# Residual rows added at each slot's down product instead of gathered by group, with fixed buffers and independent scatters

## The chip, the cores and the metric

The kernel runs on one core of one Trainium2 chip. The metric is device time in microseconds of one execution; the time given for a kernel is the median of its runs. A profile is taken of one execution, and its span is a little shorter than that execution's time.

## What is computed

One layer of a hybrid encoder over 512 tokens of width 1024, then a final RMSNorm. The first two parts (a gated mix of chunk-causal attention and pooling, then cross attention to 256 memory tokens) are dense. The third is a hierarchical mixture of experts, and this is where the change lies. Each token picks one of 4 groups and then the two best of that group's 8 experts; there are 32 experts.

```python
def hierarchical_moe(xn, w_rg, b_rg, w_re, b_re, w_gate, w_up, w_down):
    group_prob = jax.nn.softmax((xn @ w_rg) + b_rg, axis=-1)
    g_w, g_idx = lax.top_k(group_prob, 1)
    ...
    weights = g_w * e_w
    ...
    for e in range(N_EXPERTS):
        hid = jax.nn.silu(xn @ w_gate[e]) * (xn @ w_up[e])
        out = out + (hid * cw[..., e:e + 1]) @ w_down[e]
    return out

    h = h + hierarchical_moe(rms_norm(h, ffn_norm_g[l]), ...)
    return rms_norm(h, final_norm_g)
```

All is in float32. Each expert has 3 MB of weights (gate and up 2 MB, down 1 MB).

## The kernel before

The program is written out in full in Python, without loops on the chip, and each engine runs its instructions in the order in which the code issues them. On chip, memory is split into arenas (H, Q, E, G, J, C, B, R of pairs in rounded float32, F and W of plain float32). The dense stages take buffers from them; as they end, arenas are turned into slots of 1 MB for expert weights (`e_slots`, `to_raw`). Weights are fetched in the order of their use as slots come free (`e_load`, called by `e_done`), all from SyncE's queue.

The eight PSUM banks are a list: `bank()` takes the first one (L208), `put()` appends to the end (L211). The bank of a step is put back as soon as its last reader is issued; the wait for that reader is then with whoever writes the bank next.

The dense stages leave the residual h as rows of 1024 in DRAM (`H3`). The router gives lists: `src` (for each pair of experts, the tokens of its 128 places, 64 for each expert), `cws` (their weights), `srank` (the place of each within its group) and `gsrc` (for each group, the tokens of its 256 places, as two tiles t of 128). Places that hold no token are left out by the gathers' and scatters' bound.

`experts()` goes over p = 0..15, a pair of experts each (4 pairs make a group, PG = 4):

- `gather(p)` (L1534) fetches the pair's token rows from `H3` into `XG[p % 2]` with a DMA issued by GpSimd.
- `take(p)` (L1540) transposes them on TensorE, 8 blocks in two banks, into `XS[p % 2]`: the first four are copied out by VectorE (L1554), the other four by ScalarE (L1552). `rstd(p)` (L1559) squares the rows on ScalarE into two junk banks, then three small steps on GpSimd; it ends by issuing `gather(p + 2)`.
- `up(p)` (L1572) is 16 matmuls of 512 columns (two experts side by side), then SiLU on ScalarE (L1588) and a product on VectorE (L1589).
- `places(p)` (L1593) makes the one-hot matrix `OH` on GpSimd. `turn(p)` (L1598) transposes the hidden values.
- `down(p)` (L1608) is two halves n of 8 matmuls. Each half is split into a high part (ScalarE, L228) and a low part (VectorE, L229), `Y`, scaled by `cws`.
- `add(p, n)` (L1631) adds `Y` through `OH` into four banks `acc[t, n]`, which are held over the group's four pairs.

In the pair p the order is up(p), places(p), take(p + 1), add(p - 1, 0), turn(p), rstd(p + 1), add(p - 1, 1), down(p). Once in a group (p = 4, 8, 12), after add(p - 1, 1), `sums` (L1674) adds the residual rows in `HG` to the four acc banks and squares them; after down, `output` (L1682) scales by the norm and the gain and scatters the rows, one scatter for each t. `residual` (L1645) has gathered the residual rows of a group into `HG` with two DMAs after down(p) with p % 4 == 1. In the last group the residual is added by four matmuls with the identity instead (L1740), ahead of down(15), and add, square, scale and scatter follow half by half (L1750 to L1759).

## Time and profile before

| | us |
|---|---|
| median of 3 runs (lowest, highest) | 758.93 (757.88, 759.64) |
| the profiled execution | 759.05 |
| its span in the profile | 757.3 |

```profile
PE 717.7 (95%) x3603; PEld 499.9 (66%) x3604; DVE 393.9 (52%) x726; ACT 326.8 (43%) x652; POOL 183.7 (24%) x263
q1 hardware_dynamic: 30960, 144.73, 50.4%
q0 software_dynamic: 4896, 10.50, 3.8%
```

The first line gives for each engine its busy time, its share of the span and its instructions: PE is TensorE's matmuls, PEld its weight loads, DVE VectorE, ACT ScalarE, POOL GpSimd. The others give for a DMA queue its packets, megabytes and the share of the 16 DMA engines; q1 carries the weights, q0 what GpSimd issues. A matmul's end is modelled, so TensorE's busy share isn't its share of peak. The experts run from about 509 us to the end.

### The profile page before, as it was taken

To read this page: it belongs to the slowest core of one execution; us is meant where nothing else is said; L and a number is where in the kernel's file an instruction comes from. 1 tells how busy PE (TensorE), PEld (TensorE's weight loads), DVE (VectorE), ACT (ScalarE), POOL (GpSimd) and SP (SyncE) were. 2 spreads that over 40 slices of the span, in tenths; PEclk is the share of its full clock that TensorE was granted. 3 is DMA by queue.
4 is the path that set the end of the run, shared out by engine and by line. 5 is a ranking of instruction groups with operands and counts; after the bars stand their busy time and mean duration, and the time that the engine had idled before them with its cause. 6 is when DMAs were issued, how large, how long until landed. Compare 5 with 4: busy or idle time off the path is not lost. (4 is left out here: it accounts for less than half of the span.)

```text
span 757.3 us, 9883 instructions
## 1 busy us (share of the span) xinstructions
PE 717.7 (95%) x3603; PEld 499.9 (66%) x3604; DVE 393.9 (52%) x726; ACT 326.8 (43%) x652; POOL 183.7 (24%) x263
## 2 busy tenths in 40 slices
PE   8999999999999889999999999969999999998892
PEld 6787788868778668899898888833434444444330
DVE  6948444677878594886455454352224225215112
ACT  7543322656665654553444344323333424324211
POOL 4566000111111142410000002224233422512312
PEclk9999999999999999999999999979999999999997
DMA  9231323211130442256451078779999999999940
GB/s 329 85 106 28 115 87 106 79 57 39 38 112 29 151 161 106 83 166 194 141 203 57 29 310 357 251 268 346 420 419 418 419 418 418 417 417 422 412 168 36
DMA packets 38211, 159.34 MB, mean 210 GB/s; under 512 B 6544, under 2 KB 9360, under 8 KB 26640
## 3 DMA queue, kind: packets, MB, share of 16 engines
q1 hardware_dynamic: 30960, 144.73, 50.4%
q0 software_dynamic: 4896, 10.50, 3.8%
q10 hardware_dynamic: 2304, 3.45, 1.3%
q8 instruction: 29, 0.48, 0.3%
q14 instruction: 22, 0.18, 0.1%
HBM read 160.75 MB, written 6.29 MB: 221 GB/s over the span
## 5 line engine op out<-in xcount | busy, mean ns | idle before, releaser
L229 DVE SCALAR_TENSOR_TENSOR B<-b,zs,B 128x512 fp32r<-128x512 f32 x32 | 23.8, 750 | 72.2 <-ACT B L228 72.2
L1589 DVE SCALAR_TENSOR_TENSOR F<-b,r3s,F 128x256 f32<-128x256 f32 x16 | 7.7, 483 | 95.9 <-ACT F L1588 95.9
L1588 ACT ACTIVATE F<-b,r3s 128x256 f32<-128x256 f32 x16 | 7.6, 475 | 106.9 <-PE b L1580 106.9
L1636 PE MATMUL b<-B 128*128 128x512 f32 x128 | 37.7, 416 | 2.2 <-ACT B L228 1.7
L236 PE MATMUL b<-H,R 128*128 128x512 f32 x92 | 36.7, 399 | 0.0
L228 ACT ACTIVATE B<-b,zs 128x512 fp32r<-128x512 f32 x32 | 21.9, 686 | 33.2 <-PE b L1618 32.4
L1580 PE MATMUL b<-H,F 128*64 128x512 f32 x112 | 29.4, 593 | 2.0 <-DMA H<-in_we 2.0
L425 PE MATMUL b<-H,Q 128*128 128x512 f32 x120 | 27.5, 390 | 1.0 <-ACT Q L223 1.0
L751 ACT ACTIVATE F<-b,sm,cc_q 128x128 f32<-128x128 f32 (+3 forms) x32 | 19.8, 619 | 19.6 <-DVE sm L750 18.0
L1636 PEld LDWEIGHTS b<-B 128*128 128x128 f32 x128 | 21.6, 189 | 8.1 <-issue 2.6
L234 PE MATMUL b<-H,G 128*128 128x512 f32 x60 | 25.4, 423 | 1.3 <-ACT H L223 1.3
L425 PEld LDWEIGHTS b<-H,Q 128*128 128x128 f32 x120 | 22.5, 188 | 6.1 <-ACT Q L223 1.5
L1566 POOL TENSOR_SCALAR ssx<-ssx 128x1 f32<-128x1 f32 x16 | 4.1, 256 | 90.8 <-ACT b L1564 90.5
L1580 PE MATMUL b<-R,F 128*64 128x512 f32 x88 | 25.2, 593 | 0.0
L235 PE MATMUL b<-H,G 128*128 128x512 f32 x60 | 24.4, 407 | 0.7 <-DVE H L226 0.7
L1199 POOL TENSOR_TENSOR F<-F 128x512 f32<-128x512 f32 x6 | 8.1, 1342 | 66.3 <-ACT F L1197 66.3
L1580 PE MATMUL b<-Q,F 128*64 128x512 f32 x72 | 23.5, 620 | 0.0
L223 ACT ACTIVATE E<-W 128x1024 fp32r<-128x1024 f32 (+3 forms) x24 | 18.9, 797 | 9.8 <-PE b L235 3.6
L1547 PEld LDWEIGHTS b<-ident,F 128*128 128x128 f32 x128 | 13.7, 140 | 14.0 <-issue 11.4
L226 DVE TENSOR_TENSOR R<-W,R 128x1024 fp32r<-128x1024 f32 (+2 forms) x15 | 20.0, 1342 | 4.8 <-ACT R L223 4.8
L1580 PEld LDWEIGHTS b<-H,F 128*64 128x64 f32 x112 | 9.3, 137 | 18.5 <-issue 15.4
L223 ACT ACTIVATE G<-W 128x1024 fp32r<-128x1024 f32 (+3 forms) x20 | 17.7, 883 | 8.7 <-PE b L235 3.6
(619 smaller groups left out, 2243.0 us busy)
## 6 DMA issues: line engine op xcount, KB each, us to landing
W<-in_wd SPq DMA_DIRECT2D x61, 512.0 KB, 3.5
H<-in_we SPq DMA_DIRECT2D x20, 1024.0 KB, 18.1
F<-in_we SPq DMA_DIRECT2D x15, 1024.0 KB, 15.7
Q<-in_we SPq DMA_DIRECT2D x12, 1024.0 KB, 21.6
R<-in_we SPq DMA_DIRECT2D x11, 1024.0 KB, 22.5
W<-in_we SPq DMA_DIRECT2D x10, 1024.0 KB, 22.3
E<-in_we SPq DMA_DIRECT2D x5, 1024.0 KB, 20.0
G<-in_we SPq DMA_DIRECT2D x5, 1024.0 KB, 22.7
```

The source lines that it names most:

```text
L223: nc.scalar.activation(hi, src, AF.Copy)
L226: nc.vector.tensor_tensor(out=lo, in0=src, in1=hi.bitcast(F32), op=ALU.subtract)
L228: nc.scalar.activation(hi, src, AF.Copy, scale=scale)
L229: nc.vector.scalar_tensor_tensor(out=lo, in0=src, scalar=scale, in1=hi.bitcast(F32), op0=ALU.mult, op1=ALU.subtract)
L234: nc.tensor.matmul(out, l[0], r[0], start=start, stop=False)
L235: nc.tensor.matmul(out, l[0], r[1], start=False, stop=False)
L236: nc.tensor.matmul(out, l[1], r[0], start=False, stop=stop)
L425: nc.tensor.matmul(self.banks[banks[m]], w[l], x[r], start=k == 0 and l + r == 0, stop=k == 7 and l == 1)
L751: nc.scalar.activation(P[i].ap, src, AF.Exp, bias=nb[:, i:i + 1], scale=self.cq[:, i:i + 1], accum_out=sums[:, i:i + 1])
L1547: nc.tensor.transpose(self.banks[b][:, k * 128:(k + 1) * 128], x[:, f:f + 128], self.ident)
L1580: nc.tensor.matmul(self.banks[b][r], x[:, k, r], self.e_get(e, k // 4).ap[:, s], start=k == 0, stop=k == 7)
L1636: nc.tensor.matmul(self.banks[acc[t, n]], OH[p].ap[:, t * 128:(t + 1) * 128], y.ap[:, n * 512:(n + 1) * 512], start=p % PG == 0 and j == 0 ...
```

## The change

- The residual is added in `down`: after the matmuls of a half, VectorE computes bank = bank x `cws` + the pair's rows in `XG`, in place in PSUM, and the split into `Y` follows without a scale. As each token stands in two places of its group, its residual comes in twice, so the expert weights are doubled, the squares are taken of half the sum, and the final gain is halved (on GpSimd, once, after its DMA). `residual`, `sums` and the identity matmuls of the last group go; squares and scalings read acc directly.
- `gather(p + 2)` moves from the end of `rstd(p)` to the end of `down(p)`'s second half, since `XG` is read there.
- `down` is called half by half, and the order in a pair becomes up(p), places(p), add(p - 1, 0), turn(p), add(p - 1, 1), down(p, 0), output if a group closed, take(p + 1), rstd(p + 1), down(p, 1).
- There is one `XS` in place of two, at the end of F from the start; `Y`, `OH`, the gain and `HG` have fixed places. B shrinks by 1024 columns and F grows by 1024; all room that is left in F becomes weight slots, where one slot was allowed before. V is four buffers of 1024 in place of one of 4096.
- The scatters are declared independent of one another, and each is followed by a small memset of its column of `ms`.

```diff
--- before.py
+++ after.py
@@ -143,11 +143,11 @@
 
 class Kernel:
     R_N = 24 * 256
-    B_N = 16 * 256
+    B_N = 12 * 256
     Q_N = 24 * 256
     E_N = 8 * 256
     H_N = 32 * 256
-    F_N = 56 * 256
+    F_N = 60 * 256
     W_N = 16 * 256
     E_FIRST = 2
     ROWS = 6
...
@@ -329,6 +329,8 @@
 
     def build(self):
         self.ws_init()
+
+        self.XS = Buf(self.FA, 1024, at=self.F_N - 1024)
         self.d = {}
         self.no_h = self.w_pin = False
         self.w_reserve = 0
...
@@ -673,9 +675,8 @@
     def values(self):
 
         nc = self.nc
-        self.V = self.R(4 * 1024, long=True)
-        Vv = self.V.ap.rearrange("p (i h c v) -> p i h c v", i=4, h=8, c=2)
-        self.Vv = Vv
+        self.V = [self.R(1024, long=True) for _ in range(4)]
+        Vv = self.Vv = [v.ap.rearrange("p (h c v) -> p h c v", h=8, c=2) for v in self.V]
         self.w_need("v", 2)
         for i in range(4):
             b = self.bank()
...
@@ -860,7 +861,8 @@
         pv(h)
         self.tile8(self.yab[1], "ya1", rhs=self.atk, ks=range(3), nk=4)
         at_split(3)
-        self.V.free()
+        for v in self.V:
+            v.free()
         self.CE.free(), self.CO.free(), self.R1.free()
         self.tap("attn", self.at.ap)
 
...
@@ -1415,8 +1417,9 @@
             nc.vector.scalar_tensor_tensor(out=w[:, 0], in0=d, scalar=1.0, in1=gs, op0=ALU.add, op1=ALU.mult)
             nc.vector.reciprocal(w[:, 0], w[:, 0])
             nc.vector.tensor_mul(w[:, 1], w[:, 0], d)
-            nc.vector.tensor_copy(cb[:, :, :, 1], w)
-            nc.vector.tensor_tensor(out=wr, in0=w, in1=cb[:, :, :, 1], op=ALU.subtract)
+
+            nc.vector.tensor_scalar(cb[:, :, :, 1], w, 2.0, None, op0=ALU.mult)
+            nc.vector.scalar_tensor_tensor(out=wr, in0=w, scalar=2.0, in1=cb[:, :, :, 1], op0=ALU.mult, op1=ALU.subtract)
             nc.vector.tensor_copy(cb[:, :, :, 2], wr)
             nc.vector.tensor_tensor(out=cb[:, :, :, 3], in0=wr, in1=cb[:, :, :, 2], op=ALU.subtract)
 
...
@@ -1524,9 +1527,17 @@
         self.slots.append(b)
         self.e_load()
 
+    def e_rooms(self):
+
+        at = lambda n, o: Buf(self.FA, n, at=o)
+        rooms = at(1024, 1024), [at(1024, 2048), at(1024, 0)]
+        self.e_slots(self.FA)
+        return rooms
+
     def experts(self):
         nc = self.nc
-        XG, XS = self.XG, [Buf(self.BF, 1024)]
+        XG = self.XG
+        xs = self.XS.ap.rearrange("p (k c) -> p k c", k=8)
         hid, Y, OH = {}, {}, {}
         NP = NE // 2
         PG = NP // 4
...
@@ -1538,8 +1549,7 @@
                 bounds_check=511, oob_is_err=False)
 
         def take(p):
-            x = XG[p % 2]
-            v = XS[p % 2].ap.rearrange("p (k c) -> p k c", k=8)
+            x, v = XG[p % 2], xs
             for half in range(2):
                 b = self.bank()
                 for k in range(4):
...
@@ -1566,12 +1576,10 @@
             nc.gpsimd.tensor_scalar(s[:, 0:1], s[:, 0:1], 1.0 / D, EPS, op0=ALU.mult, op1=ALU.add)
             nc.gpsimd.tensor_scalar(s[:, 0:1], s[:, 1:2], 1.0 / D, s[:, 0:1], op0=ALU.mult, op1=ALU.add)
             nc.gpsimd.tensor_tensor(out=r3s[:, p:p + 1], in0=s[:, 0:1], in1=self.expo[:, :1], op=ALU.pow)
-            if p + 2 < NP:
-                gather(p + 2)
 
         def up(p):
             es = (2 * p, 2 * p + 1)
-            x = XS[p % 2].ap.rearrange("p (k c) -> p k c", k=8)
+            x = xs
             b = self.bank()
             for k in range(8):
                 s = slice((k % 4) * 512, (k % 4) * 512 + 512)
...
@@ -1592,7 +1600,7 @@
 
         def places(p):
 
-            OH[p] = self.R(256)
+            OH[p] = Buf(self.BA, 256, at=2048 + 256 * (p % 2))
             nc.gpsimd.tensor_scalar(OH[p].ap, self.iotag, self.srank[:, p:p + 1], None, op0=ALU.is_equal)
 
         def turn(p):
...
@@ -1605,25 +1613,30 @@
             nc.scalar.activation(hid[p].ap, self.banks[b][:, :256], AF.Copy)
             self.put(b)
 
-        def down(p, between=lambda n: None):
+        def down(p, n):
+
             es = (2 * p, 2 * p + 1)
-            h = hid.pop(p)
-            Y[p] = self.RP(1024)
-            for n in range(2):
-                b = self.bank()
-                for k in range(2):
-                    s = slice(k * 1024 + n * 512, k * 1024 + n * 512 + 512)
-                    for i, e in enumerate(es):
-                        r = slice(64 * i, 64 * i + 64)
-                        nc.tensor.matmul(self.banks[b][r], h.ap[:, k * 128 + 64 * i:k * 128 + 64 * i + 64],
-                                         self.e_get(e, 2).ap[:, s], start=k == 0, stop=k == 1)
-                ns = slice(n * 512, (n + 1) * 512)
-                self.split(self.banks[b], (Y[p].hi.ap[:, ns], Y[p].lo.ap[:, ns]), scale=self.cws[:, p:p + 1])
-                self.put(b)
-                between(n)
-            h.free()
-            for e in es:
-                self.e_done(e, 2)
+            h = hid[p]
+            if n == 0:
+                Y[p] = Pair(Buf(self.BA, 1024, at=0), Buf(self.BA, 1024, at=1024))
+            b = self.bank()
+            for k in range(2):
+                s = slice(k * 1024 + n * 512, k * 1024 + n * 512 + 512)
+                for i, e in enumerate(es):
+                    r = slice(64 * i, 64 * i + 64)
+                    nc.tensor.matmul(self.banks[b][r], h.ap[:, k * 128 + 64 * i:k * 128 + 64 * i + 64],
+                                     self.e_get(e, 2).ap[:, s], start=k == 0, stop=k == 1)
+            ns = slice(n * 512, (n + 1) * 512)
+            nc.vector.scalar_tensor_tensor(out=self.banks[b], in0=self.banks[b], scalar=self.cws[:, p:p + 1],
+                                           in1=XG[p % 2][:, ns], op0=ALU.mult, op1=ALU.add)
+            self.split(self.banks[b], (Y[p].hi.ap[:, ns], Y[p].lo.ap[:, ns]))
+            self.put(b)
+            if n:
+                hid.pop(p).free()
+                for e in es:
+                    self.e_done(e, 2)
+                if p + 2 < NP:
+                    gather(p + 2)
 
 
         acc = {}
...
@@ -1642,47 +1655,41 @@
         ss = [self.const([128, 2], F32, f"ss{n}") for n in range(2)]
         ms, rs = self.const([128, 2], F32, "ms"), self.const([128, 2], F32, "rs")
 
-        def residual(g):
-            for t in range(2):
-                nc.gpsimd.indirect_dma_start(
-                    out=HG[t].ap, out_offset=None, in_=self.H3,
-                    in_offset=bass.IndirectOffsetOnAxis(ap=self.gsrc[:, t, g:g + 1], axis=0),
-                    bounds_check=511, oob_is_err=False)
-
         def rows(t, n):
             return HG[t].ap[:, n * 512:(n + 1) * 512]
 
-        def square(t, n, src):
+        def square(t, n):
             b = self.bank()
-            nc.scalar.activation(self.banks[b], src, AF.Square, accum_out=ss[n][:, t:t + 1])
+            nc.scalar.activation(self.banks[b], self.banks[acc[t, n]], AF.Square, scale=0.5, accum_out=ss[n][:, t:t + 1])
             self.put(b)
             c = slice(t, t + 1)
             nc.gpsimd.tensor_scalar(ms[:, c], ss[n][:, c], 1.0 / D, ms[:, c] if n else EPS, op0=ALU.mult, op1=ALU.add)
             if n:
                 nc.gpsimd.tensor_tensor(out=rs[:, c], in0=ms[:, c], in1=self.expo[:, :1], op=ALU.pow)
 
-        def scale(t, n, src):
-            nc.vector.scalar_tensor_tensor(out=rows(t, n), in0=src, scalar=rs[:, t:t + 1],
+        def scale(t, n):
+            b = acc.pop((t, n))
+            nc.vector.scalar_tensor_tensor(out=rows(t, n), in0=self.banks[b], scalar=rs[:, t:t + 1],
                                            in1=self.gl.ap[:, n * 512:(n + 1) * 512], op0=ALU.mult, op1=ALU.mult)
+            self.put(b)
+
+        stored = []
 
         def scatter(g, t):
-            nc.gpsimd.indirect_dma_start(
+            i = nc.gpsimd.indirect_dma_start(
                 out=self.out.rearrange("b t d -> (b t) d"), in_=HG[t].ap[:, :1024], in_offset=None,
                 out_offset=bass.IndirectOffsetOnAxis(ap=self.gsrc[:, t, g:g + 1], axis=0),
                 bounds_check=511, oob_is_err=False)
 
-        def sums():
-            for t in range(2):
-                for n in range(2):
-                    b = acc.pop((t, n))
-                    nc.vector.tensor_add(rows(t, n), self.banks[b], rows(t, n))
-                    self.put(b)
-                    square(t, n, rows(t, n))
+            for before in stored:
+                self.tc.declare_no_dep(i.ins, before.ins, reason="rows of different tokens")
+            stored.append(i)
+            nc.gpsimd.memset(ms[:, t:t + 1], 0.0)
 
         def output(g):
             for t in range(2):
                 for n in range(2):
-                    scale(t, n, rows(t, n))
+                    scale(t, n)
                 scatter(g, t)
 
         self.e_slots(self.WA)
...
@@ -1708,58 +1715,41 @@
             if p == 0:
                 self.lists()
 
-                XS[0].free()
                 self.BF = None
                 self.BA = self.seg("B", F32R)
                 self.hT.free()
-                at = lambda n, o: Buf(self.FA, n, at=o)
-                XS[0] = at(1024, 0)
-                XS.append(at(1024, 1024))
-                self.gl = at(1024, 2048)
-                HG = [self.F(1024, long=True) for _ in range(2)]
+                self.gl, HG = self.e_rooms()
                 for v in HG:
                     nc.gpsimd.memset(v.ap, 0.0)
-                self.e_slots(self.FA, 1)
                 nc.sync.dma_start(self.gl.ap, self.a["g_final"].to_broadcast([128, 1024]))
+
+                nc.gpsimd.tensor_scalar(self.gl.ap, self.gl.ap, 0.5, None, op0=ALU.mult)
             places(p)
+            last = p and p % PG == 0
+            for n in range(2):
+                if p:
+                    add(p - 1, n)
+                    if last:
+                        for t in range(2):
+                            square(t, n)
+                if n == 0:
+                    turn(p)
+            down(p, 0)
+            if last:
+                output(p // PG - 1)
             if p + 1 < NP:
                 take(p + 1)
-            if p:
-                add(p - 1, 0)
-            turn(p)
-            if p + 1 < NP:
                 rstd(p + 1)
-            if p:
-                add(p - 1, 1)
-            if p and p % PG == 0:
-                sums()
-            if p == NP - 1:
-
-                for n in range(2):
-                    for t in range(2):
-                        nc.tensor.matmul(self.banks[acc[t, n]], self.ident, rows(t, n), start=False, stop=False)
-                break
-            down(p)
-            if p and p % PG == 0:
-                output(p // PG - 1)
-            if p % PG == 1:
-                residual(p // PG)
-
-        P = NP - 1
-
-        def last(n):
-            add(P, n)
+            down(p, 1)
+
+        for n in range(2):
+            add(NP - 1, n)
             for t in range(2):
-                square(t, n, self.banks[acc[t, n]])
-
-        down(P, last)
-        for t in range(2):
-            for n in range(2):
-                scale(t, n, self.banks[acc[t, n]])
-            scatter(3, t)
-        for b in acc.values():
-            self.put(b)
-        for v in XS + HG + [self.gl, self.XGB]:
+                square(t, n)
+        output(3)
+
+        self.HG = HG
+        for v in [self.XS, self.gl, self.XGB]:
             v.free()
 
 
```

Left out are the places that follow V's new shape, and the branch for crowded experts, which isn't taken with these inputs.

## Rows read from the trace of the kernel before

**Rows 1.** The page's slices: DMA engines' busy share in tenths, 40 slices of the span.
```profile
DMA  9231323211130442256451078779999999999940
```

**Rows 2.** Timeline of TensorE: start us, us, engine, line, operation; each pair's eight transposes.
```profile
532.10 1.09 PE L1547 MATMUL b<-ident,F 128*128 128x128 f32 x8
...
681.11 1.09 PE L1547 MATMUL b<-ident,F 128*128 128x128 f32 x8
...
697.75 1.09 PE L1547 MATMUL b<-ident,F 128*128 128x128 f32 x8
...
716.26 1.09 PE L1547 MATMUL b<-ident,F 128*128 128x128 f32 x8
```

**Rows 3.** Timeline of TensorE: up matmuls after a wait [idle us <- releaser].
```profile
694.17 3.65 PE L1580 MATMUL b<-H,F 128*64 128x512 f32 x14 [1.99 <-DMA H<-in_we]
...
710.99 1.12 PE L1580 MATMUL b<-E,F 128*64 128x512 f32 x1 [2.02 <-DMA E<-in_we]
```

**Rows 4.** Windows: stretch, length, busy us of PE, PEld, DVE, ACT, POOL, clock, DMA share, GB/s.
```profile
695.00:700.00 5.00, 5.00 (x27) 2.73 (x24) 1.52 (x5) 1.59 (x5) 0.00 (x0) 1.00 1.00 419
...
710.00:715.00 5.00, 4.01 (x12) 1.26 (x13) 0.00 (x0) 0.00 (x0) 0.42 (x1) 0.66 1.03 417
```

**Rows 5.** Timeline of the tail, from the last up projection's end, several engines.
```profile
730.16 1.19 PE L1636 MATMUL b<-B 128*128 128x512 f32 x4
...
732.60 3.59 PE L1740 MATMUL b<-F,ident 128*128 128x512 f32 x8
...
743.29 0.75 DVE L229 SCALAR_TENSOR_TENSOR B<-b,zs,B 128x512 fp32r<-128x512 f32 x1 [3.68 <-ACT B L228]
...
748.16 1.10 POOL L1669 DMA_INDIRECT out<-F,gsrc  x1 [0.85 <-DVE F L1665]
752.40 0.97 POOL L1669 DMA_INDIRECT out<-F,gsrc  x1 [3.14 <-issue]
```

**Rows 6.** Timeline of one ordinary pair, from its up projection on, several engines.
```profile
606.41 7.04 PE L1580 MATMUL b<-H,F 128*64 128x512 f32 x32
...
613.38 1.09 PE L1547 MATMUL b<-ident,F 128*128 128x128 f32 x8
...
614.23 1.18 PE L1636 MATMUL b<-B 128*128 128x512 f32 x4
...
614.51 1.11 DVE L1554 TENSOR_SCALAR F<-b,gcol 128x128 f32<-128x128 f32 x4
...
616.47 3.65 PE L1618 MATMUL b<-Q,F 128*64 128x512 f32 x16
...
618.46 0.69 ACT L228 ACTIVATE B<-b,zs 128x512 fp32r<-128x512 f32 x1 [1.19 <-PE b L1618]
...
619.18 0.75 DVE L229 SCALAR_TENSOR_TENSOR B<-b,zs,B 128x512 fp32r<-128x512 f32 x1 [3.55 <-ACT B L228]
```

**Rows 7.** Timeline of a pair that closes a group: first square, down's second-half weight load.
```profile
630.71 0.59 ACT L1657 ACTIVATE b<-F 128x512 f32<-128x512 f32 x1
...
631.47 0.13 PEld L1618 LDWEIGHTS b<-W,F 128*64 128x64 f32 x1 [0.40 <-ACT b L1657]
```

**Rows 8.** Groups by line and form, 540 to 720 us: busy us, mean ns | idle before.
```profile
L229 DVE SCALAR_TENSOR_TENSOR B<-b,zs,B 128x512 fp32r<-128x512 f32 x25 | 18.5, 750 | 48.9 <-ACT B L228 48.9
...
L1665 DVE SCALAR_TENSOR_TENSOR F<-F,rs 128x512 f32<-128x512 f32 x12 | 8.2, 743 | 0.0
L1678 DVE TENSOR_TENSOR F<-b,F 128x512 f32<-128x512 f32 x12 | 7.4, 681 | 0.0
```

**Rows 9.** Issues of DMA by line: engine, operation, count, KB each, median us to landing.
```profile
F<-in_g_final SPq DMA_DIRECT2D x1, 512.0 KB, 8.2
```

**Rows 10.** Timeline: the gain's DMA issue, and a comparison of 256 columns on GpSimd.
```profile
516.76 0.33 SPq L1723 DMA_DIRECT2D F<-in_g_final  x1
...
606.17 0.95 POOL L1596 TENSOR_SCALAR B<-iotag,zs 128x256 fp32r<-128x256 bf16 x1
```

**Rows 11.** The gathers' line, L1535: landing times of its 16 DMAs.
```profile
DMA to landing us min/median/max: 4.1/8.4/11.2
```

9 lines of the change are left out of this document (5 added, 4 removed).

## The prediction

> **What bounds the kernel now.** I read the page's slices first, then the timeline of TensorE over the expert pairs, then one pair on all engines, then the waits, then the tail. The slices show the DMA engines full from slice 28 to slice 37, which is the expert stage [rows 1], at about 418 GB/s [rows 4]. That alone would make DMA the bound. The starts of the eight transposes of each pair say more: from 532.10 to 681.11 us there are 11 pairs of (681.11 - 532.10) / 11 = 13.55 us, and TensorE never waits; the next two take 16.64 and 18.51 us [rows 2]. So TensorE sets the pace for twelve pairs, living on weights fetched earlier, and only in the last pairs does DMA catch it: the lost 3.09 + 4.96 us hold two waits of 2.0 us for weights and a stretch at a lower clock [rows 2 to 4]. The last up projection takes 13.90 us from the transposes before it, 0.35 over the pace, and after its end at 730.16 us comes a tail of 27.1 us of dependent work, against a span of 757.3 us [rows 2, 5].
>
> In one pair TensorE has no slack: up 606.41 to 613.38 (6.97 us), transposes 0.85, add/turn/add to 616.47 (2.24), both halves of down the rest, 3.49 of 13.55 [rows 6]. VectorE and ScalarE run beside it with long gaps, so their work is free as long as nobody on TensorE waits for it. That is what the change touches.
>
> **The bank that decides.** PSUM banks are handed out first in, first out. From the second pair on four of the eight are held by acc, so four rotate. Per pair the new order asks for: up, turn, down half 0, take half 0, take half 1, two junk banks of rstd, down half 1. The eighth request gets the bank of the fourth: down half 1 writes the bank of the first four transposes, and must wait until VectorE has copied them to XS. Before, the order was up, take, take, turn, rstd, rstd, down, down, and half 1 got the bank of turn, long empty. That the hand-out works so is in the trace: in the pair that closes a group, by the same count down half 1 gets the junk bank of the first square, and the weight load of that half waits 0.40 us for that very ScalarE instruction [rows 7].
>
> **The ordinary pair.** VectorE runs in program order, so the four copies of take stand behind the whole split of down half 0, which has grown by a step and is serial: VectorE adds the residual in PSUM, ScalarE rounds, VectorE subtracts. From the start of down half 0: 1.99 us until the first reader starts (616.47 to 618.46) [rows 6]; the new add, which the trace does not have, at 0.75 us as the multiply-and-subtract of the same shape and inputs, its nearest row, with the plain add from PSUM, 0.68, as the lower bound and the two in sequence, 1.43, as the upper one [rows 8]; ScalarE 0.69 [rows 6]; the subtraction 0.68 as the plain add [rows 8]; four copies 1.11 [rows 6]; four handovers of about 0.03 (618.46 + 0.69 to 619.18) [rows 6]. Sum 5.35 us, then half 1 may start. It would otherwise start after 1.75 (half of 3.49) + 0.85 = 2.6 us. So TensorE waits 2.75 us, and behind this wait stand half 1, the next up, and with them everything. Add/turn/add takes 2.44 without the transposes ahead of it (730.16 to 732.60, the last pair, which has none) [rows 5]. The pair becomes 6.97 + 2.44 + 5.35 + 1.75 = 16.5 us, 2.95 more. It is so in 11 pairs: +32.5 us. The first pair has all eight banks free and the last has no transposes: nothing there.
>
> **The three pairs that close a group.** Here half 1 gets an acc bank and is not held by the copies, but four scalings of 0.74 each [rows 8] are put ahead of take's copies on VectorE, and the next up needs the first copy: 4.2 us (the sum above without copies) + 3.0 for the scalings + 0.3 for a copy = 7.5 at most, 7.3 if they overlap as the four copies do. Pair: 6.97 + 2.5 + 7.3 = 16.8, +3.25 each, +9.8 us.
>
> **What this takes away.** A pair of 16.5 us is slower than DMA: 6.29 MB of weights, 0.26 of gathered and 0.13 of scattered rows take 16.0 us at 418 GB/s [rows 4]. DMA then no longer catches TensorE, and the waits of the last pairs go: -3.09 - 4.96 - 0.35 = -8.4 us [rows 2]. For the same reason the removed gathers by group (512 rows, 2.1 MB, 5.0 us of DMA at that rate) and one more weight slot in F are worth nothing. The cover is the pace of TensorE; without it they are worth 5 us (a rival, below).
>
> **The tail.** The four identity matmuls that put the residual into acc, from 732.60 on, go [rows 5]; down starts there. Half 1 of down no longer stands behind the add of half 0; against that, the split is 0.75 longer. From the end of up: down at 2.44, its second half done at 6.1, VectorE free of half 0 at 6.6, then 0.75, 0.69 and 0.75, so the last low part is there at 8.85; before it was there at 743.29 + 0.75 - 730.16 = 13.9. What follows up to the first scatter is alike (4.1 us) [rows 5], so that comes 5.0 us earlier. The second scatter now starts 4.24 us after the first, 3.14 of it idle; with the declared independence it follows the first one's 1.10 us and a small memset: 1.4 [rows 5]. Together -7.9 us.
>
> **GpSimd.** The scaling of the final gain waits there for a DMA of 8.2 us issued at 516.76, so to about 525 [rows 9, 10], and its own price lies between 0.95 (a comparison of 256 columns) and four times that [rows 10]; I take 2. Behind it stand the first places, rstd(1) and gather(2). The gather also moves past the whole pair: it is issued after half 1's residual add, 3 us after half 1 starts, and its rows are wanted 12.9 us after it, with 1.8 more before VectorE would copy anyway. Gathers land in 4.1 to 11.2 us, median 8.4 [rows 11]; 3 + 11.2 is 14.2 against 14.7. Covered, except once after the wait for the gain: +1 us (0 to 3). The doubled weights and halved gain cost nothing new: one instruction for another. The smaller B may delay a weight split in the dense stages, or the other placement of V bring one forward; the trace can't show which, and I leave 2 us either way for it, one wait of the size of those in [rows 3].
>
> **The clock.** Each pair now holds a wait of some 2.7 us. The trace has two waits of 2.0 us: after the one at 694.17 the granted clock stayed at 1.00, after the one at 710.99 it was 0.66 in 5 us, half of 2.4 GHz for a part, which costs 5 x 0.34 = 1.7 us [rows 3, 4]. The second came soon after a shorter wait. So it can go either way; I take 5 of the 14: +8.5 us, with bounds of 0 and 14 x 1.7 = 24. The Trainium skill ("TensorE: Matmul & The Clock Gate", section "A second HAM failure mode: psum-queue depth-cycling") speaks against the change here: cycling through PSUM banks in each iteration makes TensorE idle briefly between groups so often that its clock swings between its levels. By that rule, the upper bound stands.
>
> **Sum.** 757.3 + 32.5 + 9.8 - 8.4 - 7.9 + 8.5 + 1 = 792.8 us of span. The profiled execution took 759.05 us, 1.8 more than its span and 0.1 above the median of the three runs, 758.93; so 794.6 us. I forecast 794.
>
> **Rivals.** (a) The clock holds through all waits: 786. For it: the wait at 694. Chance 0.15. (b) It falls after each of the 14: 810. For it: these waits are longer than both in the trace. Chance 0.14. (c) Faster: half 1 does not wait for take's copies, because five or more banks rotate or the copies come sooner. The point from which this decides is the bank count; with it a pair stays near 13.8 us, DMA is the bound again, and the 5.0 us of traffic and the tail's 7.9 count: 759 - 12.9 + 1 = 747. Against it: the 0.40 us wait, which fits four. Chance 0.08. (d) The residual add overlaps more than I think, or the pairs gain on DMA and the waits for weights come back in part: 775 to 780, chance 0.06. (e) The independence isn't honoured and the second scatter waits as before: +2.9, inside the range. The forecast itself, with some clock drops, gets 0.57 and spans 789 to 802.
>
> **Range and chances.** Leaving out (c), part of (d) and the top of (b) with added losses: 780 to 813. Faster by over 0.2% is (c), 0.08; slower by over 0.2% (about what a measurement of this kernel can tell from no change) is the rest but 0.01.
>
> **What would show it.** Right: from the second pair on the transposes come every 16.5 us or more; the first matmul of down's second half waits 2 to 3 us each pair, released by VectorE's copies at L1554's place; no waits of the up matmuls for weights; DMA below full; tail from the last up of about 19 us with the scatters 1.4 us apart. Wrong: a pace of 13.5 to 14 us, or waits for in_we again. The steps most likely to be off are the count of clock drops, then the length of the serial split.

## The result and the profile after

The changed kernel takes 795.32 us (median of 4, 793.60 to 797.86) against 758.68 (757.88 to 759.64) for the kernel before on the same chip: ratio 1.0485, 95% interval 1.045 to 1.052. Forecast was 794, range 780 to 813. The profiled execution of after, the longest of its four, took 797.86 us with a span of 796.1; before it was 759.05 with 757.3, so 38.8 us of span are to be explained.

The page's slices come first (busy share of the DMA engines and granted TensorE clock, in tenths, 40 slices of the span).

```profile
PEclk9999999999999989999999999699999999999998
DMA  9221333202211632465510886789999899999100
```

DMA, which was full to the last slices [rows 1], is done by slice 37 and the last three slices have no weights left to fetch. No up matmul of a pair waits for weights any more: the waits of [rows 3] have no counterpart. TensorE alone sets the pace. Two turns, the small transposes once per pair, give it (timeline of TensorE: start us, us, engine, line, operation).

```profile
537.44 0.44 PE L1610 MATMUL b<-ident,F 128*128 128x128 f32 x2
...
778.26 0.44 PE L1610 MATMUL b<-ident,F 128*128 128x128 f32 x2
```

Between them lie 14 pairs: 240.82 us, 17.2 each, where 13.55 were the pace before [rows 2]. One ordinary pair shows why (timeline of several engines, in brackets the idle us before and who ended them).

```profile
643.04 1.94 PE L1627 MATMUL b<-H,F 128*64 128x512 f32 x8
644.91 1.09 PE L1557 MATMUL b<-ident,F 128*128 128x128 f32 x8
645.03 0.76 DVE L1630 SCALAR_TENSOR_TENSOR b<-b,zs,F 128x512 f32<-128x512 f32 x1 [3.34 <-PE b L1627]
645.82 0.60 ACT L223 ACTIVATE B<-b 128x512 fp32r<-128x512 f32 x1 [3.16 <-DVE b L1630]
646.45 0.69 DVE L226 TENSOR_TENSOR B<-b,B 128x512 fp32r<-128x512 f32 x1 [0.67 <-ACT B L223]
647.06 1.12 DVE L1564 TENSOR_SCALAR F<-b,gcol 128x128 f32<-128x128 f32 x4
648.23 1.94 PE L1627 MATMUL b<-H,F 128*64 128x512 f32 x8 [2.23 <-DVE F L1564]
```

Read from the top: half 0 of the down product, the next pair's transposes, and then TensorE stands for 2.23 us. VectorE adds the residual, ScalarE rounds, VectorE subtracts, and only then VectorE copies the first four transposes out of their bank (L1564); half 1 starts 0.05 us after that. In the pairs that close a group the order is another:

```profile
591.80 1.94 PE L1627 MATMUL b<-Q,F 128*64 128x512 f32 x8
...
596.67 1.94 PE L1627 MATMUL b<-Q,F 128*64 128x512 f32 x8 [1.91 <-DVE F L1672]
598.90 0.64 PE L1588 MATMUL b<-Q,F 128*64 128x512 f32 x1 [0.30 <-DVE F L1564]
```

Here half 1 waits for a scaling of the output (L1672), whose acc bank it gets, and the next up for the copies behind the scalings. In six of the 14 pairs something comes on top, the lower clock in the half behind the wait: the same eight matmuls at nearly twice the time. The granted clock is 0.54 from 578.88 to 582.44 us, where it is 1.00 for the half at 562.41 us, behind a wait of 2.25 us.

```profile
578.88 3.56 PE L1627 MATMUL b<-F 128*64 128x512 f32 x8 [2.23 <-DVE F L1564]
```

The tail, to be laid beside [rows 5]:

```profile
777.03 1.20 PE L1649 MATMUL b<-B 128*128 128x512 f32 x4
...
779.55 0.13 PEld L1627 LDWEIGHTS b<-W,F 128*64 128x64 f32 x1 [0.36 <-ACT F L1613]
...
785.07 0.69 DVE L226 TENSOR_TENSOR B<-b,B 128x512 fp32r<-128x512 f32 x1 [0.72 <-ACT B L223]
...
789.87 1.09 POOL L1679 DMA_INDIRECT out<-F,gsrc  x1 [0.85 <-DVE F L1672]
790.97 0.12 POOL L1687 MEMSET ms<- 128x1 f32 x1
791.27 0.98 POOL L1679 DMA_INDIRECT out<-F,gsrc  x1 [0.18 <-issue]
```

And one thing the prediction did not have: the experts start later. The first fence is of before, the second of after (timeline of GpSimd and TensorE): a last step of the dense part, the issue of the first gather, the first transposes.

```profile
494.46 1.02 POOL L1229 TENSOR_TENSOR r_h<-ms_h,expo 128x4 f32<-128x4 f32 x1 [6.19 <-DVE ms_h L1227]
...
504.47 1.30 POOL L1535 DMA_INDIRECT F<-H,src  x1 [4.83 <-DVE F L1414]
...
508.64 1.09 PE L1547 MATMUL b<-ident,F 128*128 128x128 f32 x8 [2.01 <-DMA F<-H,src]
```

```profile
495.22 1.02 POOL L1231 TENSOR_TENSOR r_h<-ms_h,expo 128x4 f32<-128x4 f32 x1 [6.19 <-DVE ms_h L1229]
...
507.24 1.29 POOL L1546 DMA_INDIRECT F<-H,src  x1 [6.84 <-DVE F L1424]
...
511.65 1.97 PE L1557 MATMUL b<-ident,F 128*128 128x128 f32 x8 [4.20 <-DMA F<-H,src]
```

From the dense step to the transposes it is 14.18 us before and 16.43 after; the eight transposes then take 1.97 us instead of 1.09, at the lower clock behind the longer wait. The brackets of the two gathers name VectorE, but the list of tokens is ready 8.5 us behind the dense step in both kernels. What the gather waits for is the landing of the last write of the rows that it reads (chain of work that ended last, of after):

```profile
497.54 8.80 DMA H<-F
...
507.24 4.36 DMA F<-H,src
```

In before that write is issued at 496.78 us and lands after 6.8 us; in both kernels the gather follows the landing by 0.9 us.

### The profile page after: what moved, and what is told of

Read it like the earlier page. It is cut to its first block, busy times and chain, and to the rows that moved or that the text cites. A ratio compares the mean times of both kernels' runs of the same rounds, so it can differ in the third digit from the quotient of the medians.

```text
span 796.1 us, 9833 instructions
## 1 busy us (share of the span) xinstructions
PE 732.7 (92%) x3596; PEld 498.3 (63%) x3596; DVE 409.2 (51%) x746; ACT 322.8 (41%) x652; POOL 179.9 (23%) x264
## 4 chain that ended last, share of the span: by engine, by line
PE 67%; DVE 14%; ACT 6%; issue 6%; DMA 4%; POOL 2%; ACTq 0%; SPq 0%; POOLq 0%; DVEq 0%
PE b L1588 13%; PE b L235 12%; PE b L236 12%; PE b L234 12%; PE b L1627 7%; PE b L427 3%; PE b L1649 2%; ACT B L223 2%; DMA F<-H,src 2%; DVE sm L750 2%; DVE F L1564 2%; DVE B L226 2%; DVE R L226 1%; DVE b L1630 1%; DMA H<-F 1%
## 5 line engine op out<-in xcount | busy, mean ns | idle before, releaser
L1630 DVE SCALAR_TENSOR_TENSOR b<-b,zs,F 128x512 f32<-128x512 f32 x32 | 24.2, 758 | 83.6 <-PE b L1627 83.6
L223 ACT ACTIVATE B<-b 128x512 fp32r<-128x512 f32 (+1 forms) x52 | 28.9, 573 | 91.6 <-DVE b L1630 87.9
L226 DVE TENSOR_TENSOR B<-b,B 128x512 fp32r<-128x512 f32 (+1 forms) x52 | 33.6, 658 | 24.8 <-ACT B L223 24.1
L236 PE MATMUL b<-H,R 128*128 128x512 f32 x76 | 30.3, 398 | 0.0
L1588 PE MATMUL b<-F 128*64 128x512 f32 x104 | 26.8, 632 | 0.0
L1557 PE MATMUL b<-ident,F 128*128 128x128 f32 x128 | 18.4, 289 | 8.2 <-DMA F<-H,src 8.2
L1588 PE MATMUL b<-W,F 128*64 128x512 f32 x56 | 25.3, 600 | 0.3 <-DVE F L1564 0.3
L1546 POOL DMA_INDIRECT F<-H,src x16 | 18.2, 1139 | 26.2 <-DVE b L1630 18.1
L1562 ACT ACTIVATE F<-b,gcol 128x128 f32<-128x128 f32 x64 | 18.2, 373 | 12.5 <-PE b L1557 12.5
L234 PE MATMUL b<-H,G 128*128 128x512 f32 x52 | 22.0, 424 | 1.3 <-ACT H L223 1.3
```

The lines of the kernel that those rows point to most:

```text
L223: nc.scalar.activation(hi, src, AF.Copy)
L226: nc.vector.tensor_tensor(out=lo, in0=src, in1=hi.bitcast(F32), op=ALU.subtract)
L234: nc.tensor.matmul(out, l[0], r[0], start=start, stop=False)
L236: nc.tensor.matmul(out, l[1], r[0], start=False, stop=stop)
L1557: nc.tensor.transpose(self.banks[b][:, k * 128:(k + 1) * 128], x[:, f:f + 128], self.ident)
L1588: nc.tensor.matmul(self.banks[b][r], x[:, k, r], self.e_get(e, k // 4).ap[:, s], start=k == 0, stop=k == 7)
```

## The experiments

Theory: half 1 of the down product gets the bank of the first four transposes and waits for their copies, which stand behind the split on VectorE; the clock falls behind some of these waits; what else is new in the kernel costs little. Rivals: the single buffer for transposed rows, the residual add itself, the layout. Times are medians, with the ratio to the kernel before in the same comparison.

| kernel | us | ratio, 95% |
|---|---|---|
| changed kernel | 795.32 | 1.045 to 1.052 |
| e1_bank | 771.05 | 1.0129 to 1.0182 |
| e2_xs2 | 796.35 | 1.0458 to 1.0529 |
| e3_warm | 807.07 | 1.0602 to 1.0660 |
| e3b_warm | 788.93 | 1.0376 to 1.0429 |
| e4_noadd | 780.68 | 1.0268 to 1.0340 |
| e7_layout (before + layout) | 760.32 | 1.0007 to 1.0038 |
| e9_dep (before + independence) | 756.80 | 0.9964 to 0.9994 |
| e11_start | 793.92 | 1.0436 to 1.0473 |
| e12_gain | 795.40 | 1.0471 to 1.0523 |
| e13_both | 792.99 | 1.0441 to 1.0480 |
| e8_best | 753.99 | 0.9925 to 0.9967 |
| e10_best | 750.28 | 0.9877 to 0.9931 |

### The bank: e1_bank

The junk output of the squares goes into a bank that take has just emptied, so that a pair asks for six banks and not eight.

```diff
 take:   self.put(b)
+        self.kb = b
 rstd:  -b = self.bank()
-        nc.scalar.activation(self.banks[b], ...)
-        self.put(b)
+        nc.scalar.activation(self.banks[self.kb], ...)
```

> The changed kernel with one edit: the two junk outputs of rstd go to the bank that take's second half has just left, in place of two banks from the list, so a pair asks for six banks instead of eight and down's second half gets the bank of turn. Theory (shared bank): the 2.2 us wait of down's second half goes, only the wait of the next up for the first copies stays (about 0.3 us); a pair takes 13.8 to 14.2 us, DMA becomes the bound again at the end, the clock no longer drops in the pairs, time 745 to 756 us. Rival (the wait is for the single XS or for VectorE's load, not for a bank): the pair stays above 15.5 us and the time above 780 us.

Measured 771.05. The mechanism shows at once: half 1 follows the transposes without a wait (timeline of e1_bank).

```profile
620.68 1.09 PE L1557 MATMUL b<-ident,F 128*128 128x128 f32 x8
...
621.70 1.94 PE L1626 MATMUL b<-F 128*64 128x512 f32 x8
...
634.86 1.09 PE L1557 MATMUL b<-ident,F 128*128 128x128 f32 x8
```

Such a pair takes 14.18 us instead of 16.48: 24 us of the change's loss were this one wait and what the clock lost behind it. The expected time was missed by 15 us or more, though, because with that wait gone two others come to light: the copies behind the scalings in the closing pairs, and gathers that come late behind them. The late gathers are in after too, hidden in the ordinary wait: there the transposes at 611.59 us wait 1.19 us for their rows, and half 1 behind them only 1.03 us instead of 2.23. The gather stands behind the scatters on GpSimd and is issued 5.0 us after half 1 starts, where it is 3.1 in an ordinary pair.

```profile
590.70 0.64 PE L1587 MATMUL b<-Q,F 128*64 128x512 f32 x1 [2.27 <-DVE F L1564]
...
604.81 1.09 PE L1557 MATMUL b<-ident,F 128*128 128x128 f32 x8 [2.61 <-DMA F<-H,src]
```

With the lower clock behind some of them, five of its pairs take 16.0 to 18.5 us and two more 14.5 and 15.1.

### One buffer for transposed rows: e2_xs2

Two places for the transposed rows, used in turn, as before.

```diff
+        self.XS2 = at(1024, 6144)
-            x, v = XG[p % 2], xs
+            x, v = XG[p % 2], xs[p % 2]      # xs: the places of XS and XS2
```

> The changed kernel with two buffers for transposed rows used in turn, in place of one (it costs one weight slot); banks and order as changed. Theory (shared bank): nothing changes, pairs of 16.5 us, 790 to 799 us. Rival (the one buffer makes TensorE wait): pairs under 15 us, under 775 us.

796.35, and the wait is there unchanged (timeline of TensorE of e2_xs2).

```profile
647.06 1.94 PE L1628 MATMUL b<-Q,F 128*64 128x512 f32 x8 [2.22 <-DVE F L1565]
```

The single buffer is not the cause.

### The clock: e3_warm and e3b_warm

Eight small matmuls of constant data fill the wait, into a bank that nobody uses then. In e3_warm it is the bank of the turn.

```diff
+                for i in range(8):
+                    nc.tensor.matmul(self.banks[self.tb], self.warm[:, :128], self.warm, start=i == 0, stop=i == 7)
             down(p, 1)
```

> The changed kernel with eight matmuls of 512 bf16 columns on a constant tile put on TensorE behind take's transposes, 1.7 us of work inside the 2.2 us wait, into turn's empty bank. Theory (the clock falls because TensorE is idle in the wait): pairs stay at 16.5 us but none of them runs at the lower clock, so the time falls by 5 drops of about 1.6 us, to 786 to 789 us. Rival (the drops have another cause or cost nothing): 793 to 798 us.

807.07: the experiment spoilt itself. In the three closing pairs that bank had meanwhile gone to the transposes, so that the filler itself waits 4.9 us and runs at the lower clock (timeline of TensorE of e3_warm); the pairs take 22.6 to 23.7 us.

```profile
669.96 3.57 PE L1744 MATMUL b<-warm 128*128 128x512 bf16 x8 [4.92 <-DVE F L1564]
```

In e3b_warm the filler writes the bank that half 1 is going to get later (`tb = self.free_banks[0]`).

> The changed kernel with the eight matmuls on a constant tile behind take's transposes again, now into the bank at the head of the list, which is free in every pair, also in those that close a group (e3_warm used turn's bank, which is take's own in these three pairs, so TensorE waited 4.9 us there and the clock fell). Theory (the clock falls because TensorE idles in the wait): no pair runs at the lower clock, 786 to 790 us. Rival (the drops have another cause or cost nothing): 793 to 798 us.

788.93, inside the expectation. From the start of half 0 to the start of half 1 it is unchanged (640.04 to 645.23, 5.19 us), TensorE is merely not idle meanwhile:

```profile
640.04 1.94 PE L1627 MATMUL b<-H,F 128*64 128x512 f32 x8
...
643.06 1.67 PE L1744 MATMUL b<-warm 128*128 128x512 bf16 x7
...
645.23 1.94 PE L1627 MATMUL b<-H,F 128*64 128x512 f32 x8 [0.50 <-DVE F L1564]
```

All its 14 pairs lie between 16.44 and 16.83 us, together 231.80 against 240.82 in after: 9.0 us of the change's loss were low clock in the profiled executions (the granted clock is 1.00 from 540 to 771 us here), 6.4 in the medians. The number of drops differs from execution to execution (five to seven in the profiled ones of after, e11, e12 and e13), at 1.6 us each.

### The residual add: e4_noadd

The residual is left out, and the halves are split with the weights as scale, as before.

```diff
-            nc.vector.scalar_tensor_tensor(out=self.banks[b], in0=self.banks[b], scalar=self.cws[:, p:p + 1],
-                                           in1=XG[p % 2][:, ns], op0=ALU.mult, op1=ALU.add)
-            self.split(self.banks[b], (...))
+            self.split(self.banks[b], (...), scale=self.cws[:, p:p + 1])
```

> The changed kernel without the residual add (the output lacks the residual): down's halves are split with the weights as scale, as before; banks, order and gathers as changed. Theory (the wait of down's second half is the whole serial split and the copies behind it): the wait shrinks by the add's 0.76 us, less 0.09 for the slower scaled copy, ordinary pairs 15.7 to 15.9 us in place of 16.5, the time 782 to 788 us. Rival (the added step itself is the cause): pairs near 14 us, under 770 us.

780.68, below the expectation by a little. The pair is where it was expected, 15.89 us, and the wait shrinks to 1.65 (timeline of TensorE of e4_noadd).

```profile
620.59 1.10 PE L1557 MATMUL b<-ident,F 128*128 128x128 f32 x8
...
636.48 1.09 PE L1557 MATMUL b<-ident,F 128*128 128x128 f32 x8
...
639.22 1.08 PE L1627 MATMUL b<-H,F 128*64 128x512 f32 x4 [1.65 <-DVE F L1564]
```

Its windows show the granted clock at 1.00 from 600 to 760 us (stretch, length, busy us of PE, PEld, DVE, ACT, POOL, clock, DMA share, GB/s; the last of four):

```profile
682.00:760.00 78.00, 69.71 (x326) 27.43 (x326) 17.15 (x38) 24.86 (x67) 18.66 (x34) 1.00 0.59 235
```

So the add is worth 0.59 us per pair, 8 us of the 14.6. The rest fits the clock: behind waits of 1.65 us none of its pairs shows a slow half in the profiled execution (its four executions spread over 4.5 us). The larger part of the wait, 1.65 of 2.23 us, is there without the add: it comes from the place of take between the halves and the bank count.

### The layout and the start: e7_layout, e11_start, e12_gain, e13_both

e7_layout is the kernel before with the change's region sizes, the values in four parts and the first transposed rows in F.

```diff
-    B_N = 16 * 256
+    B_N = 12 * 256
...
-    F_N = 56 * 256
+    F_N = 60 * 256
...
+        self.XS0 = Buf(self.FA, 1024, at=self.F_N - 1024)
```

> The kernel before with the memory layout of the change alone: B four blocks smaller, F four larger with a fixed buffer for transposed rows at its end, V in four pieces. Theory (the later start of the experts in the changed kernel comes from the layout): the load into J moves from 485 to about 492 us, the last part of the residual rows reaches DRAM about 2 us later, and the first transposes start at 511 to 512 us in place of 508.6; as DMA sets the end, the time grows by 0 to 3 us, 759 to 762 us. Rival (chance of that one execution): transposes at 508 to 509 us, 758 to 759 us.

760.32, and the transposes are as late as in after (timeline of TensorE of e7_layout):

```profile
511.20 1.97 PE L1548 MATMUL b<-ident,F 128*128 128x128 f32 x8 [4.05 <-DMA F<-H,src]
```

The time at which the dense part ends differs between executions, whatever the layout (that step on GpSimd starts at 492.7 to 496.6 us). Counted from it the transposes start after 14.2 and 15.1 us in before and e9, which have the old layout, and after 16.3 to 16.5 in after, e1, e2, e7, e8 and e12, which have the new one. So the late start comes with the layout, 1.2 to 2.3 us. It goes by the landing of the rows' last write. A weight load into region J is issued 3.2 us ahead of the dense step in after (492.01 us) and 9.6 ahead of it in before (484.87), and in five us while that write is under way the DMA engines' share is 1.02 in after (500 to 505 us) and 0.69 in before (499 to 504). That the later load makes the write slower fits all this, but was not tried by itself. In e7 the end is 1.7 us later only, as the last pairs still wait for weights there, and for less time (0.68, 1.41 and 1.34 us, where before has 1.99 and 2.02).

What the start is worth in the changed kernel was tried by giving e11_start the old region sizes.

```diff
-    B_N = 12 * 256
+    B_N = 16 * 256
...
-    F_N = 60 * 256
+    F_N = 56 * 256
...
-        self.XS = Buf(self.FA, 1024, at=self.F_N - 1024)
...
+        self.XS = Buf(self.BF, 1024)          # first pair; later pairs: at(1024, 6144) in F
```

> The changed kernel with the region sizes and the transposed rows of the first pair as before (16 and 56 instead of 12 and 60 in the regions B and F, the rows of the first pair in B, the later ones in one place of F); all else is the change. Theory (the start of the experts is 4.1 us late by the layout, of which 3.0 in the wait for the first gather and 1.1 at the lower clock behind that longer wait, and nothing later takes it back since DMA is not the bound of the changed kernel): the first transposes of the experts at 508 to 509 us instead of 511.65, pairs of 16.5 us with low-clock halves as before, time 790.5 to 792.5. Rival (the late start is taken back by other waits, as in the kernel before with the layout alone, where 2.6 us of delay cost 1.7): 793.5 to 795.5.

793.92: 1.4 us less than after, and the rival's figure. From the dense step to the first transposes it is 15.45 us, half of the delay, and on to the first turn of the 14 pairs 40.1 for 42.2 in after: 2.1 us won. But the third gather hangs on something else (timeline of GpSimd, then of TensorE, of e11_start):

```profile
528.04 2.78 POOL L1728 TENSOR_SCALAR F<-F 128x1024 f32<-128x1024 f32 x1 [5.71 <-DMA F<-in_g_final]
...
533.26 1.18 POOL L1547 DMA_INDIRECT F<-H,src  x1 [0.21 <-issue]
```

```profile
541.49 1.79 PE L1558 MATMUL b<-ident,F 128*128 128x128 f32 x8 [2.68 <-DMA F<-H,src]
```

GpSimd stands for the final gain, halves it for 2.78 us, and only then issues the gather for which the transposes at 541.49 wait. e12_gain moves that instruction behind the second pair's down product, with the layout of the change.

```diff
-                nc.gpsimd.tensor_scalar(self.gl.ap, self.gl.ap, 0.5, None, op0=ALU.mult)
...
             down(p, 1)
+            if p == 1:
+                nc.gpsimd.tensor_scalar(self.gl.ap, self.gl.ap, 0.5, None, op0=ALU.mult)
```

> The changed kernel with one instruction moved: the halving of the final gain on GpSimd comes after the second pair's down product and its gather, not before the first places. Theory (the gather for the third pair is late because GpSimd stands for the landing of the gain and then 2.79 us at the halving, so that it is issued at 533.56 and its rows are wanted by 540.7): the gather is issued by 530 us, the waits of 1.66 and 0.78 us in front of and behind the third transposes go, the second pair takes 16.5 us or, with a clock drop, 18.0 instead of 18.45; time 793 to 795. Rival (the wait is set by the transfer alone, which competes with the weights): the rows land no earlier, 795 to 796.

The gather is issued at 529.05 and the waits of 1.66 and 0.78 us that after has there go, as the theory said; the time does not move (795.40, in the rival's range and just outside the theory's). The ordinary wait, 2.18 us, stands in their place, the half behind it runs at the lower clock as it does in after, and the second pair takes 18.24 us instead of 18.45. e13_both is e11 with the same move.

> The changed kernel with both: region sizes and transposed rows of the first pair as before, and the halving of the gain moved behind the second pair's gather. Theory (an earlier start was worth only 1.4 us because the third gather hung on the gain's landing, which did not move with it): with both the start's 3 to 4 us come through, 789.5 to 792. Rival (some other wait takes the start's gain back): 792.5 to 794.5, no better than either alone.

792.99, 2.3 us less than after; that is inside the rival's range and above the theory's. The third transposes do not wait for rows, the second pair takes 16.54 us, and from the dense step to the first turn it is 39.97 us for 42.22, 2.25 won. So the theory holds in kind, with a start of 2.2 us and not of 3 to 4; since the intervals of e13 and after overlap, it rests on the trace more than on the times. In e11 and e13 the transposes still start 15.4 us behind the dense step, for 14.2 in before. That need not be the layout's: e9, which keeps the old layout, has 15.1, and e10 below, with the region sizes of e11, 14.3.

### The scatters: e9_dep

The kernel before with the independence of the scatters (and their memset) alone.

```diff
-            nc.gpsimd.indirect_dma_start(
+            i = nc.gpsimd.indirect_dma_start(
...
+            for old in stored:
+                self.tc.declare_no_dep(i.ins, old.ins, reason="rows of different tokens")
+            stored.append(i)
...
```

> The kernel before, with the one part of the change that concerns the end of the kernel: the scatters are declared independent of each other (and the small memset that goes with it); gathers by group, layout and pace of the pairs as before. Theory (the tail of the prediction): the second half of the last scatter no longer waits for the landing of the first, its issue falls 1.4 us behind the first instead of 4.24 us, and the time is some 2.9 us lower, 755 to 757 us. Rival (the declaration is not honoured, or the last scatter lands no earlier because its rows are ready no earlier): the second issue stays 4.2 us behind the first, 758 to 760 us.

756.80, ratio 0.9979 (0.9964 to 0.9994). The second scatter follows 1.41 us after the first instead of 4.24 (timeline of GpSimd of e9_dep).

```profile
750.66 1.10 POOL L1669 DMA_INDIRECT out<-F,gsrc  x1 [0.85 <-DVE F L1665]
751.77 0.12 POOL L1676 MEMSET ms<- 128x1 f32 x1
752.07 0.98 POOL L1669 DMA_INDIRECT out<-F,gsrc  x1 [0.18 <-issue]
```

The 2.8 us are in the trace; the time shows 1.6, with 2.7 at the end of its interval.

### A version that beats both: e8_best, e10_best

e8_best is e1 with a third buffer for gathered rows, so that gathers start a pair earlier (the third one ahead of the gain's DMA), and the scalings of the output behind take's copies.

```diff
-                if p + 2 < NP:
-                    gather(p + 2)
+                if p + 3 < NP:
+                    gather(p + 3)          # into XG[p % 3]
...
-            if last:
-                output(p // PG - 1)
             if p + 1 < NP:
                 take(p + 1)
                 rstd(p + 1)
+            if last:
+                output(p // PG - 1)
```

> e1_bank with two edits for what it still waits for: a third buffer for gathered rows, so that gather(p + 3) is issued where gather(p + 2) was, and the scalings and scatters of a closed group after take and rstd of the next pair. Theory (e1_bank's 771 us are its pairs of 14.2 us plus the closing pairs' 2.3 us waits behind the scalings, late gathers of up to 2.6 us and the clock drops behind both): pairs of 14.2 us throughout, no wait for H3's rows, 754 to 760 us. Rival (DMA or the clock holds it back whatever the order): 764 to 772 us.

753.99, all 14 pairs at 14.15 to 14.19 us: the waits that e1 uncovered were what kept it at 771; what each of the two edits is worth was not tried. e10_best adds the old layout, as e11 has it, and gives the first four copies to ScalarE.

```diff
-                    if half:          # ScalarE copies, else VectorE
+                    if not half:
```

> e8_best with the memory layout of before (B 16 and F 56 blocks, the buffer for transposed rows in B for the first pair and in F after it) and with the two halves of take swapped between the engines: ScalarE copies the first four transposes, VectorE the others. Theory: the first transposes start at 508 to 509 us again, the up projection no longer waits 0.4 us for its first copies, pairs of 13.6 to 13.9 us, 746 to 753 us, under the kernel before; the last pairs may wait for weights. Rival: as e8_best, 754 to 760 us.

750.28, ratio 0.9877 to 0.9931. The swap of the copies gave nothing: the pairs stay at 14.17, where 13.6 to 13.9 were expected. So the 3.7 us come with the layout, 2.9 of them by the first turn (39.1 us from the dense step for 42.0). TensorE has no idle stretch left there (a window of e10_best, columns as in e4).

```profile
640.00:680.00 40.00, 39.85 (x188) 16.07 (x186) 13.12 (x27) 11.93 (x32) 11.22 (x18) 1.00 1.02 418
```

Its pair is 0.62 longer than 13.55. By the starts of its operations add/turn/add takes 2.54 us instead of 2.24, since no transposes cover the turn's copies; the two halves of down 1.87 + 1.77 instead of 3.49; and the transposes between them 1.02 instead of 0.85 [rows 6].

## Why the prediction was right

The account of the span, in the prediction's terms. The start is taken to the end of the second up projection (532.10 before, 536.19 after), the tail from the end of the last.

| step | predicted | measured |
|---|---|---|
| 11 ordinary pairs | +32.5 | 11 x (16.49 - 13.55) = +32.3 |
| 3 closing pairs | +9.8 | 3 x (16.67 - 13.55) = +9.4 |
| clock, and the gather behind the gain | +8.5, +1 | 240.82 - 11 x 16.49 - 3 x 16.67 = +9.4 |
| waits for weights gone | -8.4 | none left: -8.4 |
| tail | -7.9 | 19.1 instead of 27.1: -8.1 |
| start of the experts | 0 (2 either way) | +4.1 |
| sum | +35.5 | +38.7 |

**The bank that decides** was right, and it is shown, not only argued: e1 takes the extra requests away and the wait goes, while e2 leaves it. The count of four rotating banks was taken from a wait of 0.40 us [rows 7].

**The ordinary pair** came out at 16.48 us for 16.5 predicted. Its parts erred by little, and against each other. From the start of half 0 to that of half 1 it was 5.19 us (5.35), mostly as ScalarE's rounding without a scale took 0.60 and not 0.69. The wait was 2.23 (2.75), as the transposes start 3.32 us before half 1 rather than 3.6 and run for 1.09 where 0.85 was taken. Add/turn/add took 2.55 (2.44). The new add, bounded from 0.68 to 1.43 and taken at 0.75, took 0.76; without it the pair is 0.59 shorter (e4).

**The closing pairs** had the right price by a path that was not quite the one described. The prediction had half 1 free and the next up waiting for copies behind four scalings; in fact half 1 also waits, 1.91 us, since the acc bank that it gets is one that a scaling has to empty. From the start of half 0 to the next up it is 7.10 us (7.3).

**The clock** was the least certain term: five drops of 1.7 us, a count that was a guess between 0 and 14, and six of about 1.6 came in the profiled execution. The only warning in before was that one of two waits of 2.0 us was followed by the lower clock; the "shorter wait" ahead of it is the other one, of 1.99 us, 17 us earlier. e3b shows that the drops come from the idle time and what they cost: with TensorE kept busy none is left, and 9.0 us go. The Trainium skill ("TensorE: Matmul & The Clock Gate", section "A second HAM failure mode: psum-queue depth-cycling") says that short idle times between groups of matmuls make the clock swing. The trace agrees in kind; taken as a drop in every pair it would have given 24 us, and the trace has 6 drops of 14.

**What it takes away.** The waits for weights went, as said. "DMA below full" held by little: its share is 0.96 to 1.00 up to 720 us, at 382 to 405 GB/s, where before had 1.02 and 418, and it falls far only when nothing is left to fetch. That fits the 16.0 us of traffic against 16.5 us of pace. As no up projection waits for weights, fewer bytes were worth nothing. Whether they count in e8 and e10, where a pair takes 14.17 us, was not tried. The gathers were not "covered" behind two of the three closing pairs (rows 1.19 us late, as they were issued 5.0 us and not 3 behind the start of half 1), which cost nothing here since half 1 would have waited as long.

**The tail** was right in each number: first scatter 12.84 us after the last up's end (18.0 - 5.0 = 13.0 predicted), the last low part 8.73 (8.85), the second scatter 1.40 behind the first (1.4). Rival (e) is out, by e9 too.

**What was mis-sized** is the start. The prediction named the layout, could not see its sign, and left 0 with 2 us either way; it is +4.1, of which 0.8 is the spread of the dense part's end, 2.2 the gather that waits for a later landing, and 1.1 comes behind it, 0.88 of that in the eight transposes at the lower clock. The row that would have warned is the 2.01 us wait for the first gather in the trace of before: a wait at that place says that whatever lands late ahead of it moves the start. The gain's price on GpSimd was 2.79 for 2 taken, and it began at 528.34 and not 525. That made the third gather late, which cost next to nothing (e12), as the pair would have lost about as much to its ordinary wait and the clock. That the forecast of 794 is 1.3 us from the median is partly luck: the account of the profiled execution is 3.2 us over the sum, and the median execution is 2.5 us shorter than the profiled one. The four executions of after took 793.6 and 794.1 us at a mean granted clock of 0.974, and 796.6 and 797.9 at 0.969, which fits two drops fewer in the first two; they were not traced.

Rival (c) had the lever and nearly the pair (14.17 us once the bank is free, for 13.8), but not the time: the closing pairs and the late gathers had to be mended too before 754 came out (e8).

## What to carry to other kernels

When buffers are handed out first in, first out, count the requests of one round of the loop: moving a step can give a matmul a buffer that is still being emptied instead of one that is long empty, and the wait then shows on the fast engine, although the slow engine has gaps everywhere. A junk output also counts as a request; here writing it into a buffer that is free anyway gave back 24 of the 37 us. When the first wait goes, expect the next ones to appear, and look for them in the trace before judging the idea by its time.

## What was not expected of the hardware

The clock's price depends on more than idle time in sum. With waits of 2.23 us (1.91 in closing pairs, 2.44 in two parts in the second pair) six of 14 pairs had a half at the lower clock (rows like 3.56 us for 1.94); with waits of 1.65 us, three quarters as long, none had it in the execution that was traced (e4), nor behind the three of 2.1 to 2.4 us in two parts that stand among them. Which pairs it hits is much the same from kernel to kernel: counted from the second pair as 1, they are 1, 3, 6, 9, 12 and 14 in after, e2 and e12, and every third, 2, 5, 8, 11 and 14, in e13, whose pairs wait as long.

Cutting a run of 64-column matmuls in two by eight 128-column transposes cost 0.15 us on the matmuls and 0.17 on the transposes, with nothing waiting between them (e10 against [rows 6]).

A gather of a pair's rows lands in 4.3 to 9.9 us, median 8.3, in after, much as before ([rows 11]), although the DMA engines move 382 to 405 GB/s up to 720 us, and not 418, and little from 740 us on.
